# First layer's expert products: whole forms in place of half forms, and one nested branch in place of two

## The chip, the cores and the metric

One core of a Trainium2 chip runs the whole program in one launch. The metric is the device time of the launch in microseconds (us); the times shown are medians of repeated executions, and the profile is that of one further execution.

## The reference, cut to what matters

A backbone of two layers over 512 rows of width 1024 (256 context rows and 256 rows of the stream). Each layer is a mixer followed by a mixture of 16 experts, of which each token takes two:

```python
def moe(t, w_router, b_router, w1, w3, w2):          # t: (N, 1024); N = 512 in the first layer, 256 in the second
    ...                                               # gates: (N, 16), two of them not zero in a row
    y = jnp.zeros(t.shape, jnp.float32)
    for e in range(N_EXPERTS):
        h = jax.nn.silu(t @ w1[e]) * (t @ w3[e])      # w1, w3: 1024 x 512
        y = y + gates[:, e:e + 1] * (h @ w2[e])       # w2: 512 x 1024
    return y.astype(t.dtype)
```

All in float32. Only the experts of the first layer (l = 0) are changed.

## The kernel before

**Stages.** The program runs the first mixer, the first layer's experts, the second mixer and the second layer's experts, one after the other. In the trace the first layer's experts run from 538 to 893 us.

**An expert's tokens.** A router counts the tokens of each expert on the chip and writes into `cni` how many groups of 32 each expert has (`nu`). The tokens of an expert are gathered 64 to a unit: the first unit always, the second if `nu > 2` (more than 64 tokens), the third if `nu > 4` (more than 128). GpSimd (POOL) gathers the rows into `xg` (units one and two) and `xo` (unit three) and scatters the results `ys` and `yo` to `y_d`.

**Products.** `up` multiplies a unit's transposed rows by the gate and up matrices into one PSUM bank `hp`: 16 matmuls of 64 columns by 512. `down` multiplies the hidden rows by the down matrix into `yp`: 8 matmuls. `up32` and `down32` are the half forms for a unit that holds 32 tokens or fewer: 32 and 16 matmuls of 32 by 256, which fill the four column groups of the array. `zeros` clears a bank with one bf16 matmul, so that the later code may read a bank whose unit is empty. `unit_up` and `unit_down` do the third unit: transposes of `xo`, the product, the hidden rows in `yo`, then transposes, the product and the copy to `yo`.

**Branches.** `nu` is read into a register of TensorE (PE), ScalarE (ACT) and VectorE (DVE), and `tc.If` makes each of these engines branch by itself. Both sides of every branch stand in each engine's code, whether they run or not; an engine that skips a side jumps over it. One expert of the first layer has these branches in the PE code: L1733 and L1734 (third unit's up), L1724 and L1725 (second unit's up), L1749 and L1750 (second unit's down), L1756 and L1757 (copies, empty on PE), L1767 and L1768 (third unit's down).

**The loop.** For each expert `n`, in the order `SEQ`, `first_up(n)` and then `then_down(n - 1)` are written; in the first layer the order of an engine's instructions is left to a scheduler, which mixes them. PE, ACT, DVE and POOL each run their own list in order.

**Weights.** Each expert has six tiles of 1 MB. SyncE (SP) issues the loads (L1410) into a ring of 14 tiles (`wx`, `wm`, `w`): a load waits until PE has used up the tile that lay in its place, and for the load issued three before it. The ring thus holds two experts and a third of the next.

The lines of the loop that the change does not touch, but that the argument uses:

```python
                    nus[n] = count(SEQ[n], PE, ACT, DVE)
                    hs = first_up(n, xTs.pop(0), nus[n])
...
                    hT = hpose(bank(), before, "hT")
...
                    xTs.append(xpose(xg[(n + 1) % 3]))
...
                    then_down(n - 1, hT, nus[n - 1])
```

## Time and profile before

| | |
|---|---|
| median of 3 runs | 1534.67 us (1533.02 to 1538.39) |
| the profiled execution's own time | 1538.6 us |
| its span, first to last instruction | 1536.8 us |
| mean granted clock of TensorE | 0.909 of full speed |
| first layer's experts | 538 to 893 us of the span |

The span is cut into stages below. Busy time of PE counts matmuls, and "idle before" is the time in which an engine did nothing ahead of an instruction, with what ended it. `PEq` names PE's own sequencer, which is where a branch runs; "issue" is a wait for nothing that the profile shows. The queue `instruction` of the DMA table is what the engines' code is fetched with.

### The profile page before, as it was taken

The page shows a single profiled execution, that of the slowest core. Times are in us where ns is not written, and L with a number is a line of the kernel's source. Part 1 is how long each engine was busy: PE and PEld are TensorE (multiplying, and loading weights), DVE is VectorE, ACT ScalarE, POOL GpSimd, SP SyncE. Part 2 cuts the span into 40 slices and gives each one's busy share as a digit, 9 for nine tenths or more (in the row PEclk, how much of TensorE's full clock was granted, in tenths as well). Part 3 has the DMA queues.
Part 4 walks back from the last instruction along what each step waited for, and adds up shares of the span by engine and source line. Part 5 has one row for each costly group of instructions (what it writes and reads, how often), then busy time and mean ns, then how long its engine had stood idle before and what let it go on. Part 6 is the DMA issues. An engine that isn't in the chain of part 4 may idle for free. (4 is left out here: it accounts for less than half of the span.)

```text
span 1536.8 us, 21725 instructions
## 1 busy us (share of the span) xinstructions
PE 1242.1 (81%) x8336; PEld 779.4 (51%) x8336; DVE 641.0 (42%) x1581; ACT 408.3 (27%) x838; POOL 100.7 (7%) x135
## 2 busy tenths in 40 slices
PE   4899999999979278788798824899987588888873
PEld 2667887567669223333243303888647234443441
DVE  4333323455447711211112128835556445444445
ACT  2223223344343010111111113443122233333222
POOL 0000000100010210111110010000010000000000
PEclk9899999999679689999899965899998799999997
DMA  8565655600020897899988242321274879998831
GB/s 277 185 205 166 231 182 195 186 1 1 1 83 15 297 339 283 296 362 334 302 287 292 103 138 82 118 80 61 76 267 164 314 283 385 355 336 321 320 122 57
DMA packets 152139, 311.20 MB, mean 202 GB/s; under 512 B 7580, under 2 KB 39516, under 8 KB 151944
## 3 DMA queue, kind: packets, MB, share of 16 engines
q1 hardware_dynamic: 146176, 296.44, 55.2%
q0 software_dynamic: 4608, 8.59, 2.1%
q10 hardware_dynamic: 1160, 3.48, 0.6%
q8 instruction: 133, 2.18, 0.6%
q14 instruction: 62, 0.51, 0.1%
HBM read 303.24 MB, written 9.44 MB: 203 GB/s over the span
## 5 line engine op out<-in xcount | busy, mean ns | idle before, releaser
L364 PE MATMUL mm<-wh,uT 128*128 128x256 f32 (+2 forms) x960 | 194.7, 298 | 7.7 <-ACT uT L345 4.5
L364 PEld LDWEIGHTS mm<-wh,uT 128*128 128x128 f32 x960 | 159.9, 199 | 20.9 <-issue 9.9
L364 PE MATMUL mm<-wl,uT 128*128 128x256 f32 (+2 forms) x480 | 142.2, 297 | 3.8 <-DVE wl L347 3.7
L1554 PE MATMUL mm<-wx,xT 128*64 128x512 f32 x392 | 121.0, 632 | 20.0 <-PEq L1733 18.6
L364 PEld LDWEIGHTS mm<-wl,uT 128*128 128x128 f32 x480 | 95.5, 199 | 5.6 <-DVE wl L347 5.1
L347 DVE TENSOR_TENSOR wl<-w,wh 128x2048 fp32r<-128x2048 f32 (+3 forms) x33 | 53.8, 1646 | 71.3 <-ACT wh L345 45.8
L1554 PEld LDWEIGHTS mm<-wx,xT 128*64 128x64 f32 x392 | 37.8, 144 | 75.1 <-issue 71.6
L246 PE MATMUL mm<-w,sT 128*32 128x512 f32 x384 | 59.5, 632 | 11.8 <-DVE sT L210 10.3
L345 ACT CAST wh<-w 128x2048 fp32r<-128x2048 f32 (+3 forms) x33 | 45.8, 1388 | 67.0 <-DMA w<-in_w_in_even_dram 52.9
L364 PE MATMUL mm<-uT,wh 128*128 128x512 f32 (+1 forms) x208 | 58.9, 370 | 4.9 <-ACT wh L345 4.9
L1582 PE MATMUL mm<-wx,hT 128*64 128x512 f32 x168 | 51.8, 609 | 12.3 <-PEq L1767 7.2
L1567 ACT ACTIVATE hs<-mm 64x512 f32<-64x512 f32 x32 | 18.8, 589 | 151.2 <-PE mm L1554 115.7
L364 PE MATMUL mm<-wo,mx 128*128 128x256 f32 x384 | 51.4, 293 | 5.7 <-ACT wo L345 3.5
L364 PEld LDWEIGHTS mm<-wo,mx 128*128 128x128 f32 x384 | 48.7, 198 | 6.6 <-ACT wo L345 3.9
L1554 PE MATMUL mm<-w,xT 128*64 128x512 f32 x104 | 45.1, 650 | 1.1 <-issue 0.9
L1554 PE MATMUL mm<-wm,xT 128*64 128x512 f32 x80 | 41.3, 698 | 5.2 <-PEq L1733 5.2
L1608 DVE COPY ys<-mm 64x512 f32<-64x512 f32 x18 | 12.5, 693 | 78.9 <-ACT ys L1608 67.8
L364 PEld LDWEIGHTS mm<-uT,wh 128*128 128x128 f32 (+1 forms) x208 | 36.3, 184 | 14.0 <-ACT wh L345 5.2
L1568 DVE TENSOR_TENSOR hs<-hs,mm 64x512 f32<-64x512 f32 x32 | 22.1, 690 | 49.7 <-ACT hs L1567 49.3
L1494 PE MATMUL ac<-h,sel 128*64 128x512 f32 x104 | 27.3, 644 | 18.7 <-DVE sel L1485 18.7
L1117 PE MATMUL tr<-cst,yk 128*128 128x128 f32 x32 | 6.0, 350 | 44.4 <-ACT yk L1110 44.4
L1554 PE MATMUL tr<-wx,xT 128*64 128x512 f32 x152 | 39.0, 595 | 3.3 <-PE ac L1510 2.8
(472 smaller groups left out, 2341.2 us busy)
## 6 DMA issues: line engine op xcount, KB each, us to landing
w<-in_w_ada_dram SPq DMA_DIRECT2D x48, 1024.0 KB
wx<-in_w_expert_gate_dram SPq DMA_DIRECT2D x46, 1024.0 KB
wx<-in_w_expert_up_dram SPq DMA_DIRECT2D x44, 1024.0 KB
wx<-in_w_expert_down_dram SPq DMA_DIRECT2D x39, 1024.0 KB
w<-in_w_expert_down_dram SPq DMA_DIRECT2D x15, 1024.0 KB
w<-in_w_in_even_dram SPq DMA_DIRECT2D x13, 1024.0 KB
w<-in_w_expert_up_dram SPq DMA_DIRECT2D x12, 1024.0 KB
wm<-in_w_expert_down_dram SPq DMA_DIRECT2D x10, 1024.0 KB
```

What stands on the lines that cost most here:

```text
L246: nc.tensor.matmul(ps[32 * g:32 * g + 32, :], sT[:, k, :], ws[k // 4][:, k % 4, :], start=k < 4, stop=k >= 4, skip_group_check=True, tile_ ...
L345: nc.scalar.copy(hi, src)
L347: nc.vector.tensor_tensor(lo, src, hi.bitcast(FP), op=OP.subtract)
L364: nc.tensor.matmul(ps, lhs(i, k), rhs(j, k), start=(k == 0 and n == 0), stop=(k == nk - 1 and n == 2))
L1117: nc.tensor.transpose(ps[:, k * 128:(k + 1) * 128], y[:, kk_ * 128:(kk_ + 1) * 128], ident)
L1494: nc.tensor.matmul(xp[i * 64:i * 64 + 64, :], sel[:, b, :], u[:, i * 512:(i + 1) * 512], start=b == 0, stop=b == len(us) - 1, skip_group_c ...
L1554: nc.tensor.matmul(hp[i * 64:i * 64 + 64, :], xT[:, k, :], ws[2 * i + k // 4][:, k % 4, :], start=k == 0, stop=k == 7, skip_group_check=Tr ...
L1567: nc.scalar.activation(hs, hp[0:64, :], AF.Silu)
L1568: nc.vector.tensor_tensor(hs, hs, hp[64:128, :], op=OP.mult)
L1582: nc.tensor.matmul(yp[n * 64:n * 64 + 64, :], hT[:, k, :], ws[4 + k // 2][:, k % 2, n * 512:(n + 1) * 512], start=k == 0, stop=k == 3, ski ...
L1608: (nc.vector.tensor_copy if n else nc.scalar.copy)(ys[:, ns], yp[rs_, :])
```

## The change

In the first layer, `up32` and `down32` are no longer used: a unit is either left out or multiplied in whole. `zeros(hp[1])` is now done for every expert ahead of the branch. One branch `nu > 2` holds the second unit's product and, inside it, a branch `nu > 4` with the third unit; the down side has the same shape, with the copies in the same branch. The second layer's branches are the same as before, written inside its own `else`. `unit_up` and `unit_down` keep their half form as an option that the first layer no longer uses.

```diff
@@ first_up
                 hp = [(bank if l else mmt)() for _ in range(2)]
+                hs = e2p.tile([128, 512], FP, name="hs", tag="hs", bufs=2)
                 if l == 0:
+
+                    zeros(hp[1])
                     up(hp[0], xT[0], ws)
+                    with tc.If(nu > 2):
+                        up(hp[1], xT[1], ws)
+                        with tc.If(nu > 4):
+                            unit_up(n % 2, e, 2, ws)
                 else:
...
-                with tc.If(nu > 2) as c1:
-                    with tc.If(nu > 3) as c2:
-                        up(hp[1], xT[1], ws)
-                    with c2.Else():
-                        up32(hp[1], xT[1], ws)
-                with c1.Else():
-                    zeros(hp[1])
-                hs = e2p.tile([128, 512], FP, name="hs", tag="hs", bufs=2)
-                if l == 0:
-                    with tc.If(nu > 4) as c1:
-                        with tc.If(nu > 5) as c2:
-                            unit_up(n % 2, e, 2, ws)
...
-                            unit_up(n % 2, e, 2, ws, True)
...
@@ then_down
                     down(yp[0], hT[0], ws)
                     rows_out(ys[0:64, :], yp[0])
-                    downs()
-                    outs(nu)
-                    with tc.If(nu > 4) as c1:
-                        with tc.If(nu > 5) as c2:
+                    with tc.If(nu > 2):
+                        down(yp[1], hT[1], ws)
+                        rows_out(ys[64:128, :], yp[1])
+                        with tc.If(nu > 4):
                             unit_down(n % 2, e, 2, ws)
-                        with c2.Else():
-                            unit_down(n % 2, e, 2, ws, True)
```

How this moves PE's list is seen at the second expert (`n = 1`). Before, its second product stands in these rows (`mm` is a PSUM bank, `wx` a weight tile, `zb` the tile of zeros, x16 the number of equal instructions in a row):

```order
L1724 COMPARE_AND_BRANCH
L1725 COMPARE_AND_BRANCH
L1554 MATMUL mm<-wx,xT 64x512 x16
L1725 UNCONDITIONAL_BRANCH
L1458 LDWEIGHTS zb
L1458 MATMUL mm<-zb 128x256
L1562 MATMUL mm<-wx,xT 32x256 x32
L1725 UNCONDITIONAL_BRANCH
L1458 LDWEIGHTS zb
L1458 MATMUL mm<-zb 128x512
L1724 UNCONDITIONAL_BRANCH
```

The third unit's up stands a few rows ahead of that, in a branch of its own (`xo` is the third unit's gathered rows, `xT_4827` and `xT_4857` its transposes):

```order
L1733 COMPARE_AND_BRANCH
L1734 COMPARE_AND_BRANCH
L1651 MATMUL ac<-cst,xo 128x64 x8
L1554 MATMUL tr<-wx,xT_4827 64x512 x16
L1734 UNCONDITIONAL_BRANCH
L1651 MATMUL ac<-cst,xo 128x64 x8
L1458 LDWEIGHTS zb
L1458 MATMUL ac<-zb 128x256
L1562 MATMUL ac<-wx,xT_4857 32x256 x32
L1734 UNCONDITIONAL_BRANCH
L1733 UNCONDITIONAL_BRANCH
```

In the changed kernel the same expert's rows, the clearing matmul first, are these (L1722 is now `nu > 2`, L1724 `nu > 4`):

```order
L1458 LDWEIGHTS zb
L1458 MATMUL mm<-zb 128x512
L1554 MATMUL mm<-wx,xT 64x512
L1626 UNCONDITIONAL_BRANCH
L1554 MATMUL mm<-wx,xT 64x512 x2
L1710 TENSOR_LOAD cni_3546
L1722 COMPARE_AND_BRANCH
L1724 COMPARE_AND_BRANCH
L1651 MATMUL ac<-cst,xo 128x64 x8
L1554 MATMUL ac<-wx,xT_4710 64x512 x16
L1724 UNCONDITIONAL_BRANCH x2
L1554 MATMUL mm<-wx,xT 64x512 x16
```

An expert of 64 tokens or fewer jumped twice on the up side, over 8 + 16 + 8 + 32 product matmuls and then over 16 + 32; it now jumps once, over 8 + 16 + 16. On the down side of the first expert, the changed kernel has these rows of PE (L1765 is `nu > 2`, L1768 `nu > 4`, `hT` the transposed hidden rows):

```order
L1582 MATMUL mm<-wx,hT 64x512
L1765 COMPARE_AND_BRANCH
L1768 COMPARE_AND_BRANCH
L1574 MATMUL ac<-cst,yo 128x64 x4
L1582 MATMUL tr<-wx,hT 64x512 x4
L1582 MATMUL tr<-wm,hT 64x512 x4
L1768 UNCONDITIONAL_BRANCH x2
L1582 MATMUL mm<-wx,hT 64x512 x4
L1582 MATMUL mm<-wm,hT 64x512 x4
L1765 UNCONDITIONAL_BRANCH x2
```

There was a jump over 8 + 16 matmuls (L1749), an empty branch (L1756) and a jump over 4 + 8 + 4 + 16 (L1767); there is now one jump over 4 + 8 + 8.

## Rows read from the trace of the kernel before

**Rows 1.** The experts' stage: busy us (count) of PE, PEld, DVE, ACT, POOL; clock, DMA, GB/s.
```profile
538.00:893.00 355.00, 294.68 (x1672) 115.66 (x1672) 64.35 (x99) 44.74 (x81) 39.84 (x43) 0.94 0.81 281
```

**Rows 2.** Waits of PE, 538 to 893 us: total, times, longest.
```profile
PE mm L1554 <- PEq L1733: 23.8, 9, 5.5
...
PE mm L1582 <- PEq L1767: 8.5, 12, 2.4
PE mm L1458 <- issue: 4.8, 2, 3.2
PE mm L1582 <- PEq L1733: 4.4, 1, 4.4
...
PE mm L1582 <- PEq L1749: 2.5, 5, 0.6
...
PE mm L1458 <- DVE ys L1608: 2.1, 1, 2.1
...
PE mm L1554 <- DMA wx<-in_w_expert_down_dram: 0.7, 1, 0.7
```

**Rows 3.** Branches on PE's sequencer: shortest/median/longest ns, first and last start.
```profile
L1733 PEldq COMPARE_BRANCH  x16: 65/2106/6497, 539.2 to 871.5; - x16
...
L1724 PEldq COMPARE_BRANCH  x16: 70/1418/5247, 540.8 to 865.0; - x16
...
L1767 PEldq COMPARE_BRANCH  x16: 65/219/3797, 570.1 to 889.6; - x16
```

**Rows 4.** PE in order of time: start, us, what, count, [idle before].
```profile
577.00 2.64 PE L1582 MATMUL mm<-wm,hT 128*64 128x512 f32 x5 [4.42 <-PEq L1733]
...
585.47 1.06 PE L1554 MATMUL mm<-w,xT 128*64 128x512 f32 x1
...
610.44 3.66 PE L1562 MATMUL ac<-wx,xT 128*32 128x256 f32 x64 [0.57 <-DVE xT L1653]
...
625.13 0.59 PE L1554 MATMUL mm<-wm,xT 128*64 128x512 f32 x1
...
625.56 0.59 PE L1554 MATMUL mm<-wm,xT 128*64 128x512 f32 x1
...
649.44 1.93 PE L1590 MATMUL ac<-w,hT 128*32 128x256 f32 x32 [1.41 <-DVE hT L1576]
```

**Rows 5.** PE matmuls by shape, 538 to 893 us: count, busy, mean ns.
```profile
L1554 PE MATMUL mm<-wx,xT 128*64 128x512 f32 x392 | 121.0, 632 | 20.0 <-PEq L1733 18.6 <-DMA wx<-in_w_expert_down_dram 0.7 <-ACTq L1733 0.3
...
L1554 PE MATMUL mm<-w,xT 128*64 128x512 f32 x104 | 45.1, 650 | 1.1 <-issue 0.9
L1554 PE MATMUL mm<-wm,xT 128*64 128x512 f32 x80 | 41.3, 698 | 5.2 <-PEq L1733 5.2
...
L1458 PE MATMUL mm<-zb 128*128 128x512 bf16 x10 | 4.1, 409 | 7.5 <-issue 4.8 <-DVE ys L1608 2.1 <-PE mm L1554 0.7
...
L1458 PE MATMUL mm<-zb 128*128 128x256 bf16 x4 | 1.1, 283 | 0.0
...
L1458 PE MATMUL ac<-zb 128*128 128x256 bf16 x2 | 0.6, 283 | 0.0
```

**Rows 6.** DMA queues, 538 to 893 us: packets, MB, share of 16 engines.
```profile
q1 hardware_dynamic: 38010, 91.26, 72.4%
...
q8 instruction: 49, 0.80, 0.9%
```

**Rows 7.** The longest of the waits of SP's loads, 538 to 893 us.
```profile
SPq L1410 <- PE mm L1554: 83.9, 39, 10.6
```

**Rows 8.** Two stretches in which loads follow each other closely; columns as in rows 1.
```profile
660.00:680.00 20.00, 14.99 (x61) 5.74 (x59) 3.46 (x5) 2.34 (x4) 3.66 (x4) 0.91 1.04 382
...
700.00:720.00 20.00, 16.29 (x121) 6.57 (x120) 3.46 (x5) 2.34 (x4) 2.84 (x3) 1.00 0.97 324
```

**Rows 9.** The last load of the stage, from SP's list in order of time.
```profile
847.09 0.37 SPq L1410 DMA_DIRECT2D w<-in_w_expert_down_dram  x1
```

**Rows 10.** The same kind of wait in the second layer's experts, 1205 to 1500 us.
```profile
PE ac L1458 <- issue: 12.8, 5, 4.0
```

## Prediction

> **What bounds the kernel now.** I first cut the span into stages. The change touches one of them, the first layer's experts, 355 us long: PE is busy 295 us there, DVE 64, ACT 45, and the DMA engines 81% of the time at 281 GB/s [rows 1]. So it is PE or the weights, and the reader is to see which of them waits for the other. The list of PE's waits answers: for weights PE waited once, 0.7 us [rows 2]. The loads wait the other way round, 83.9 us in 39 waits for PE to finish the up products that read the tile in their place [rows 7]. PE sets the pace, the DMA engines have some room.

> PE is not busy all that time, and its waits have one author. 23.8 and 4.4 us end at branch L1733, 8.5 at L1767, 2.5 at L1749 [rows 2]. Two further entries are the same thing under another name: the clearing matmul L1458 stands right behind branch L1724, and its 4.8 us "issue" and the 2.1 us put down to a DVE copy are times in which L1724 was still being taken. Together 46.1 us. The branch view shows what a branch costs on PE's sequencer: 0.2 us in the median at L1767, but 2.1 us in the median and 6.5 at worst for L1733, 5.2 at worst for L1724 [rows 3]. These are the jumps over the longest pieces of code.

> What a long jump waits for is seen in the DMA view. In the trace a float32 product matmul is two matmul and two weight-load records, a transpose one of each. An expert's up side lays down 16 + 64 + 16 + 2 + 128 = 226 such instructions in the third unit's branch and 64 + 2 + 128 + 2 = 196 in the second's; the down side 32 + 64 = 96 and 8 + 32 + 8 + 64 = 112; what always runs is 16 + 64 + 8 + 32 = 120. That is 750 an expert, 12000 in the stage, against 49 packets of 0.80/49 MB = 16 KB on the queue that fetches code [rows 6]: one fetch for each 245 instructions, so the whole code is fetched in its order, run or not. 49 fetches in 355 us are one in 7.2 us, and a jump pair L1733, L1724 moves 400 instructions on, more than a whole fetch, in a few microseconds. PE then stands until the next piece is there.

> [...]

> **Part one: the products grow.** Half forms ran six times: four second units and two third units, seen in the six half clears of a bank [rows 5], one in each of six experts. A half up takes 3.66 us by the timeline for its 64 records, say 3.6, and 0.28 for its clear [rows 4, 5]. In a whole one, two records run side by side and pairs start 0.43 us apart (625.13 and 625.56) [rows 4], so 16 pairs take 6.9 us. A half down took 1.93 us [rows 4], a whole one is 8 pairs, 3.4 us. So each of the six costs 6.9 - 3.9 + 3.4 - 1.9 = 4.5 us more, 27 us in all. `zeros` now also runs in the six experts that did without a whole clear: 6 x 0.41 = 2.5 us [rows 5]. Sum +29.5 us of PE at full clock, all on the path, since PE sets the pace. The copies of the whole forms (two in place of four) are ACT's and DVE's, which are busy 45 and 64 us of 355 [rows 1]; I price them at nothing, and at one 0.7 us copy at the very end of the stage if that cover is gone.

> **Part two: the jumps shrink.** In the changed list an expert lays down 16 + 64 + 64 = 144 instructions in the up branch, 8 + 32 + 32 = 72 in the down branch and 122 that always run, 338 in all, 5400 in the stage: by 245 a fetch some 22 fetches, one in 15 us, against a worst wait of 6.5. An up-side jump moves 144 on, a down-side jump 72, and with the always-run instructions between them a pair stays below one fetch. So a jump finds its target there, nearly always. What stays is the price of a near jump: some 0.2 us for each of 16 at L1722 (the median of L1767 is 0.22 [rows 3]) and 0.5 us at L1765 for the ten experts that skip it (L1749's 2.5 us in 5 [rows 2]), 8 us together. Gain: 46 - 8 = 38 us. Bounds: 46 if even these vanish, and 0 if the jumps go on waiting as before.

> **Part three: the clock.** [...] The means of the three up groups, 632, 650 and 698 ns [rows 5] against 590 undisturbed (0.59 in the timeline), give (392 x 42 + 104 x 60 + 80 x 108)/470 = 67 records at half clock, each holding its slot 0.215 us longer: 14 us. The granted clock of 0.94 [rows 1] bounds it above: 12% of 355 us at half clock, 43 us, costs at most 21. The few records at the stage's start stay slow; the down products, which I leave out, have some too. Value taken: 14, of 0 to 21.

> **Sum.** 29.5 - 38 - 14 = -22.5 us. The profiled execution took 1538.6 us, its span 1536.8; it would be 1516. The median of the runs shown is 1534.7, 0.25% lower, and I make the forecast on that: 1512. Ahead of the stage only the first clearing matmul moves, into a time in which PE waits for the router; behind it nothing changes its order and all starts earlier by as much. But the second layer's code lies at other addresses, and its five waits of this kind, 12.8 us [rows 10], may as well be 7 or 19.

> **Rivals.**
> - *More than the sum.* All 46 us of waits and all 21 of the half clock go: 29.5 - 46 - 21 = -37.5, 1497 us. For it speaks that every long idle of PE is of this kind; against it, that a branch always costs something.
> - *The weights become the pace.* The stage moves 281 x 355 = 99.8 MB; the last load is issued at 847 us [rows 9], lands near 852, and 41 us of work follow. At 382 GB/s [rows 8] the traffic would fit into 261 us and would end at 799, far ahead of need; at 324 GB/s, the slacker stretch, into 308 us, to 846: a gain of 6 us, 1529. That stretch, too, has loads waiting for PE, so it is a low reading.
> - *Half of the waits stay*, because single jumps still fall on the edge of a fetched piece soon after another one: 23 of 46 and 7 of 14 go, 29.5 - 23 - 7 = 0, 1534 us.
> - *Distance is not the cause* (the other side). If the branch at the head of the up side waits for being taken at that place, whatever it jumps over, L1722 inherits L1733's 28.2 us; only L1724's 6.9, 5 of the down side's 11 and 3 of the half clock go: 29.5 - 14.9 = +14.6, 1549 us. It decides as soon as L1722's median stays near 2 us. The pattern of code fetches speaks against it. [...]

> **How the numbers follow.** The sum as it stands 0.52 (own range 1503 to 1521), more than the sum 0.15, weights 0.12, half the waits 0.12, distance not the cause 0.09. A measurement of this kernel can tell about 0.3%, 4.6 us, from no change. Faster than 1530: 0.52, 0.15, 0.09 of the weights and 0.02 of the halves, 0.78. Within 0.3%: 0.11. Slower: 0.11. The range runs from below the second case to near the half-waits case, 1494 to 1531; it leaves out the last case and the outer parts of its neighbours, some 0.2.

> **What the changed profile would show.** Packets on the code queue in the stage fall from 49 to about 22. L1722 and L1765 stand in PE's branch view with medians of a few tenths; PE's waits put down to branches fall from 46 to about 8 us. No L1562 or L1590 is left in the stage, and there are six more whole products of each kind and 16 clears. The stage's granted clock rises above 0.97. Its length falls from 355 to about 332 us, SP's waits for PE shrink, and PE still waits for weights only some microseconds. The prediction is wrong if L1722 keeps waits of 3 to 6 us (then 1534 or 1549), if PE's waits for DMA grow beyond 15 us (then 1529), or if the stage shrinks as said and the second layer's experts give it back at their own branches.

## The result, and the profile after

The changed kernel takes 1498.84 us in the median (1497.33 to 1500.31), beside 1536.53 us (1533.02 to 1539.77) for the kernel before: a ratio of 0.9755, 95% interval 0.9727 to 0.9783, or 37.7 us less. A second, later comparison gave 0.9778 (0.974 to 0.9816). The forecast was 1512, 22.5 us less. The profiled execution took 1497.3 us, with a span of 1495.5.

The stage of the first layer's experts, from the start of its first transpose to the end of its last product (busy us and count of PE, PEld, DVE, ACT, POOL; then clock, DMA share, GB/s):

```profile
534.20:857.20 323.00, 308.73 (x1383) 116.13 (x1383) 63.10 (x92) 43.34 (x73) 39.90 (x43) 0.99 0.87 308
```

The window of [rows 1] is 0.7 us wider than the stage; cut in the same way, 538.5 to 892.8 us, the stage before is 354.3 us long with PE busy for 294.7. So it is 31.3 us shorter now. PE's idle time, length minus busy, goes from 59.6 to 14.3 us (-45.3), while its busy time grows from 294.7 to 308.7 (+14.0). The granted clock rises from 0.94 to 0.99. PE's waits in the stage (total, times, longest):

```profile
PE tr L1545 <- DMA xg<-u_d,io: 9.3, 1, 9.3
PE tr L1545 <- DVE hT L1576: 3.5, 10, 0.3
...
PE mm L1554 <- PEq L1722: 1.3, 7, 0.3
PE mm L1582 <- PEq L1765: 1.2, 7, 0.2
PE mm L1582 <- ACTq L1768: 0.8, 1, 0.8
...
PE mm L1582 <- PEq L1768: 0.5, 3, 0.2
...
PE mm L1554 <- PEq L1724: 0.3, 2, 0.2
```

The first line is the wait for the first gathered rows, ahead of the stage's first transpose. The five entries at branches sum to 4.1 us, where [rows 2] had 46.1, and no wait for a weight tile is left. The branches themselves on PE's sequencer (shortest/median/longest ns):

```profile
L1722 PEldq COMPARE_BRANCH  x22: 70/181/417, 536.6 to 834.9; - x22
...
L1724 PEldq COMPARE_BRANCH  x8: 65/196/419, 579.2 to 828.8; - x8
...
L1765 PEldq COMPARE_BRANCH  x22: 65/180/431, 556.5 to 853.6; - x22
```

The longest is 0.43 us, where [rows 3] had 6.5. The up and down products by shape (count, busy, mean ns):

```profile
L1554 PE MATMUL mm<-wx,xT 128*64 128x512 f32 x504 | 143.3, 600 | 1.6 <-PEq L1722 0.8 <-PEq L1724 0.3 <-PE mm L1554 0.2
...
L1554 PE MATMUL mm<-w,xT 128*64 128x512 f32 x120 | 47.0, 595 | 0.3 <-PEq L1722 0.2 <-issue 0.2
L1554 PE MATMUL mm<-wm,xT 128*64 128x512 f32 x80 | 34.6, 596 | 0.5 <-PEq L1722 0.3 <-issue 0.2
```

The means of 632, 650 and 698 ns [rows 5] are now 595 to 600: almost no record runs at half clock, a granted clock of 0.50, which stands in 5 of the stage's 323 us (1.00 in the rest). The code queue in the stage, packets and MB, and SP's waits for its loads:

```profile
q8 instruction: 23, 0.38, 0.5%
```

```profile
SPq L1410 <- DMA wx<-in_w_expert_down_dram: 48.1, 16, 5.1
SPq L1410 <- DMA wx<-in_w_expert_up_dram: 42.7, 18, 3.0
SPq L1410 <- PE mm L1554: 36.6, 19, 9.5
```

23 code packets stand in place of 49 [rows 6]. The loads wait less for PE (36.6 us against 83.9 in [rows 7]) and now mostly for earlier loads, at 308 GB/s against 281. They keep up, though with less room.

**What lies outside the stage.** The profiled spans differ by 41.3 us. By the first and last PE work of each part, the experts' stage gives 31.3 of them (354.3 to 323.0 us). It starts 4.3 us earlier (538.5 to 534.2), and the stretch from its end to the second layer's experts is 6.6 us shorter (311.8 to 305.2); the second layer's experts take 310.1 us against 309.6. Neither gain stands in edited code. A second profile of the changed kernel has its stage start at 529.5 and that stretch at 308.2, so both move by 3 to 5 us between executions of one kernel.

### The profile page after: what moved, and what is told of

Same layout as the page of the kernel before. It is cut to its first block, busy times and chain, and to the rows that moved or that the text cites. A ratio compares the mean times of both kernels' runs of the same rounds, so it can differ in the third digit from the quotient of the medians.

```text
span 1495.5 us, 20846 instructions
## 1 busy us (share of the span) xinstructions
PE 1240.5 (83%) x8048; PEld 766.7 (51%) x8048; DVE 639.0 (43%) x1575; ACT 408.7 (27%) x832; POOL 101.2 (7%) x135
## 5 line engine op out<-in xcount | busy, mean ns | idle before, releaser
L364 PE MATMUL mm<-wh,uT 128*128 128x256 f32 (+2 forms) x960 | 189.7, 293 | 7.9 <-ACT uT L345 4.8
L364 PEld LDWEIGHTS mm<-wh,uT 128*128 128x128 f32 x960 | 155.6, 194 | 21.0 <-issue 9.9
L1554 PE MATMUL mm<-wx,xT 128*64 128x512 f32 x504 | 143.3, 600 | 1.6 <-PEq L1722 0.8
L1554 PEld LDWEIGHTS mm<-wx,xT 128*64 128x64 f32 x504 | 44.4, 137 | 66.7 <-issue 65.9
L1582 PE MATMUL mm<-wx,hT 128*64 128x512 f32 x192 | 54.1, 597 | 1.7 <-PEq L1765 0.9
L1554 PE MATMUL mm<-w,xT 128*64 128x512 f32 x120 | 47.0, 595 | 0.3 <-PEq L1722 0.2
L1554 PE MATMUL tr<-wx,xT 128*64 128x512 f32 x152 | 39.0, 595 | 3.2 <-PE ac L1510 2.8
L364 PE MATMUL mm<-uT,wl 128*128 128x512 f32 (+1 forms) x104 | 37.8, 367 | 2.3 <-DVE wl L347 2.3
```

Of the source, the lines that this page charges most:

```text
L364: nc.tensor.matmul(ps, lhs(i, k), rhs(j, k), start=(k == 0 and n == 0), stop=(k == nk - 1 and n == 2))
L1554: nc.tensor.matmul(hp[i * 64:i * 64 + 64, :], xT[:, k, :], ws[2 * i + k // 4][:, k % 4, :], start=k == 0, stop=k == 7, skip_group_check=Tr ...
L1582: nc.tensor.matmul(yp[n * 64:n * 64 + 64, :], hT[:, k, :], ws[4 + k // 2][:, k % 2, n * 512:(n + 1) * 512], start=k == 0, stop=k == 3, ski ...
```

## Experiments

The theory: a branch costs what PE waits for code, and that grows with the code that an expert lays down, run or not. A first rival says that the merged, nested branch is what helps; a second that it is the number of branches. The table gathers PE's side of the stage, each from one windows row between the start of the stage's first transpose and the end of its last product. The code length is the count of PE's instructions in the kernel's list, both sides of every branch included.

| kernel | PE instructions in the stage's code | code packets | stage, us | PE busy | PE idle |
|---|---|---|---|---|---|
| before | 12,766 | 49 [rows 6] | 354.3 | 294.7 | 59.6 |
| changed | 5,788 | 23 | 323.0 | 308.7 | 14.3 |
| e1, whole forms, old branches | 5,871 | 22 | 324.1 | 306.4 | 17.7 |
| e2, half forms, nested branch | 12,640 | 49 | 349.1 | 302.2 | 46.9 |
| e3, changed + dead code | 12,638 | 49 | 403.0 | 341.2 | 61.8 |
| e5, changed + less dead code | 7,935 | 31 | 351.4 | 317.4 | 34.0 |

**Whole forms under the old branches (e1).** Against the kernel before, the first layer's half forms are taken out, and the separate branches and the `Else` with the clear stay:

```diff
+                if l == 0:
+                    with tc.If(nu > 2) as c1:
+                        up(hp[1], xT[1], ws)
+                    with c1.Else():
+                        zeros(hp[1])
+                else:
...
-                    with tc.If(nu > 4) as c1:
-                        with tc.If(nu > 5) as c2:
-                            unit_up(n % 2, e, 2, ws)
-                        with c2.Else():
-                            unit_up(n % 2, e, 2, ws, True)
+                    with tc.If(nu > 4):
+                        unit_up(n % 2, e, 2, ws)
```

> Whole products as in the change, but the two separate branches of the kernel before (second unit with its clear in an else, third unit in a branch of its own, copies in a branch of their own). Theory 'length of code jumped over': the stage's code is as short as in the change (about 5900 instructions), so the long waits are gone here too; 1497 to 1504 us, PE's branch waits under 12 us. Rival 'the one nested branch does it': most of the gain is missing, 1515 to 1535 us, with waits of some microseconds at the branches.

Measured: 1499.26 us (1491.53 to 1504.73) beside 1531.21, ratio 0.9804 (0.9751 to 0.9858), which overlaps the changed kernel's. The up side's branches:

```profile
L1739 PEldq COMPARE_BRANCH  x18: 70/208/413, 533.0 to 833.4; - x18
...
L1725 PEldq COMPARE_BRANCH  x22: 70/178/342, 534.7 to 833.2; - x22
```

Two separate branches an expert on the up side, and none takes longer than 0.42 us. Over the whole stage PE's waits at branches sum to 11.0 us, 8.0 of them in ten waits of at most 1.0 us at the third unit's branch on the down side (L1772), where the changed kernel has 4.1 in all. The nesting may save some of that, but the time is the same without it: it is not what the change lives on.

**The nested branch with the half forms kept (e2).** The other half of the change alone, shown against the changed kernel:

```diff
                     with tc.If(nu > 2):
-                        up(hp[1], xT[1], ws)
+                        with tc.If(nu > 3) as c2:
+                            up(hp[1], xT[1], ws)
+                        with c2.Else():
+                            up32(hp[1], xT[1], ws)
                         with tc.If(nu > 4):
-                            unit_up(n % 2, e, 2, ws)
+                            with tc.If(nu > 5) as c3:
+                                unit_up(n % 2, e, 2, ws)
+                            with c3.Else():
+                                unit_up(n % 2, e, 2, ws, True)
```

> The one nested branch of the change, but with the half forms of the kernel before inside it. Theory 'length of code jumped over': 12600 instructions of code as before, one jump of 434 for an expert of 64 tokens or fewer; the waits stay (35 to 60 us of PE idle at branches, 45 or more fetches of code), and the cheaper products come back: 1525 to 1545 us. Rival 'nested branch': fewer branches and cheaper products, 1470 to 1505 us.

Measured: 1536.9 us (1529.1 to 1545.8) beside 1531.21, ratio 1.0042 (1.0012 to 1.0071): no gain. Branches on PE's sequencer, then PE's waits:

```profile
L1722 PEldq COMPARE_BRANCH  x16: 70/4661/7196, 535.3 to 853.0; - x16
...
L1771 PEldq COMPARE_BRANCH  x16: 70/420/6638, 569.0 to 876.4; - x16
```

```profile
PE mm L1554 <- PEq L1722: 22.7, 8, 5.0
...
PE mm L1582 <- PEq L1771: 4.9, 1, 4.9
PE mm L1554 <- PEq L1727: 4.9, 4, 2.0
```

The same branch L1722 that takes 0.18 us in the changed kernel takes 4.7 us in the median here, where it jumps over 434 instructions in place of some 152. (In the one profile the stage is 5.2 us shorter than before, while the median is 0.4% longer. In that profile the second layer's experts, whose source is the same, take 317.4 us in place of 309.5.)

**Dead code in the changed kernel (e3).** A half up and half down product of the second and third unit stand behind a branch that is never taken. Every product and clear that runs is the changed kernel's:

```diff
                     with tc.If(nu > 2):
                         up(hp[1], xT[1], ws)
                         with tc.If(nu > 4):
                             unit_up(n % 2, e, 2, ws)
+                    with tc.If(nu > 15):
+                        up32(hp[1], xT[1], ws)
+                        unit_up(n % 2, e, 2, ws, True)
```

(and the same with `down32` and `unit_down` on the down side)

> The change with the half forms put back as code that never runs (a branch nu > 15 behind each side, which no expert of these inputs takes), so that products and order are those of the change and the code is as long as before (12600 instructions). Theory 'length of code jumped over': 40 to 60 us of waits at the new branch come back, and the half clock behind them; 1540 to 1570 us, slower than the kernel before. Rival 'running the half forms is what cost' (their four column groups, their copies): 1499 to 1504 us.

Measured: 1578.04 us (1570.23 to 1590.68) beside 1531.21, ratio 1.029 (1.0227 to 1.0353): some 80 us more than the changed kernel took, for code that never runs, and above the 1540 to 1570 us expected. The profiled execution was the slowest of the four (1590.68 us). The stage, PE's waits in it, and its code packets:

```profile
535.20:938.20 403.00, 341.16 (x1383) 123.00 (x1383) 63.11 (x92) 44.17 (x75) 40.04 (x43) 0.93 0.72 248
```

```profile
PE mm L1554 <- PEq L1726: 32.8, 12, 8.1
PE mm L1582 <- PEq L1773: 9.7, 13, 2.5
...
PE mm L1554 <- issue: 7.8, 2, 4.1
PE mm L1582 <- issue: 2.4, 1, 2.4
```

```profile
q8 instruction: 49, 0.80, 0.8%
```

Idle time is back at 61.8 us, near the 59.6 of before, with the same 49 code packets. The busy time also grows, by 32.4 us against the changed kernel, for the same 1383 matmul records. This growth is what the expectation had too small. PE in order of time behind one such wait (start, us, what, count, [idle before]) shows why:

```profile
643.35 1.08 PE L1554 MATMUL mm<-wm,xT 128*64 128x512 f32 x1 [6.74 <-PEq L1726]
643.36 1.12 PE L1554 MATMUL mm<-wx,xT 128*64 128x512 f32 x1
644.23 1.06 PE L1554 MATMUL mm<-wm,xT 128*64 128x512 f32 x1
...
648.50 0.74 PE L1554 MATMUL mm<-w,xT 128*64 128x512 f32 x1
...
649.07 0.59 PE L1554 MATMUL mm<-w,xT 128*64 128x512 f32 x1
```

For 5 us after the wait a record takes 1.06 us in place of 0.59. In the trace of the kernel before, records of 1.06 us stand where the granted clock is 0.50 (578.00 to 579.50 us) and records of 0.59 us where it is 1.00 (624 to 627 us). So this wait of 6.7 us costs about 2.5 us more behind it (an estimate: half of those 5 us). It is the part that a count of the waits alone leaves out.

**Less dead code (e5).** Only the half up product of the second unit stands behind the never-taken branch:

```diff
+                    with tc.If(nu > 15):
+                        up32(hp[1], xT[1], ws)
```

> The changed kernel with a shorter piece of code that never runs: in each of the first layer's 16 experts a half up product of the second unit behind a branch that is never taken (132 instructions of PE by my count, jumped over 16 times, beside the 151 of the changed kernel's own up-side jump); the stage's code grows from some 5800 to some 7900 instructions, about 32 fetches in place of 23. What is computed is that of the changed kernel. Code-length theory: the two jumps of an expert together pass more than one fetched piece (284 against 245), so part of the waits comes back, but each jump is short of one piece: PE's waits at branches in the stage 10 to 30 us against the changed kernel's 3, the time 1510 to 1540 us on a chip where the kernel before takes 1531 to 1537. Rival one, that only a jump of more than a whole piece costs (as 280 did in the earlier run with dead code): within 5 us of the changed kernel, 1494 to 1504. Rival two, that one more branch an expert is what costs, whatever its length: the same as the earlier run with dead code, 1570 to 1590.

Measured: 1526.13 us (1518.73 to 1529.41) beside 1533.79, ratio 0.9945 (0.9919 to 0.9971), 27 us more than the changed kernel on the same chip. Both rivals fall. The stage, the two jumps of the up side, their waits, and the code packets:

```profile
532.40:883.80 351.40, 317.40 (x1383) 116.99 (x1383) 63.10 (x92) 43.37 (x74) 39.83 (x43) 0.97 0.81 283
```

```profile
L1722 PEldq COMPARE_BRANCH  x22: 70/182/367, 534.8 to 861.1; - x22
...
L1726 PEldq COMPARE_BRANCH  x16: 208/270/4632, 536.5 to 861.3; - x16
```

```profile
PE mm L1554 <- PEq L1726: 18.2, 12, 5.0
...
PE mm L1554 <- issue: 2.7, 2, 1.7
```

```profile
q8 instruction: 31, 0.51, 0.6%
```

L1722 jumps over the same 151 to 154 instructions as in the changed kernel and is as quick. L1726 jumps over only 132 to 134, fewer than L1722, and yet holds the waits: it comes right behind, and the two together move 284 instructions on, more than one packet (256 instructions here, 7,935 in 31). In e3 a branch at the same place jumps over 280 instructions in place of 132, and its waits are 32.8 us in place of 18.2. In e1, too, two up-side jumps follow each other, over 83 and 66 instructions, and PE's waits at them stay at 0.3 us or less. What counts in these runs is the code passed in a short time, not one branch's distance and not the number of branches.

**The second layer's second unit whole (e4).** The same recipe on the other layer, on top of the change:

```diff
-                    with tc.If(nu > 2) as c1:
-                        with tc.If(nu > 3) as c2:
-                            up(hp[1], xT[1], ws)
-                        with c2.Else():
-                            up32(hp[1], xT[1], ws)
-                    with c1.Else():
-                        zeros(hp[1])
+                    zeros(hp[1])
+                    with tc.If(nu > 2):
+                        up(hp[1], xT[1], ws)
```

(and `down` and `rows_out` alone under `nu > 2` in `downs` and `outs`)

> The change, and in the second layer the second unit without half form too, its bank cleared ahead of the branch; the jump over it falls from 198 instructions to 66. Theory 'length of code jumped over': the waits behind that branch (12.8 us in the kernel before) and their half clock go, one product of a half form grows by 4.5 us: 1483 to 1494 us. Rival: those waits are another cost of a branch there, or are hidden by the loads: 1499 to 1504 us.

Measured: 1490.32 us (1485.8 to 1491.62) beside 1531.21, ratio 0.9725 (0.9673 to 0.9778), against the change's 0.9755 in another comparison: the intervals overlap. So both ran again, side by side on one chip:

> The changed kernel itself, for a comparison with the next on one chip. Expected 1497 to 1501 us where the kernel before takes 1531 to 1537.

> The kernel with the second layer's second unit made whole, beside the changed kernel on one chip. If its gain is real (its waits of 8.2 us behind that branch are gone): 7 to 10 us below the changed kernel. If the earlier 8.5 us came from the chips and the executions: within 3 us of it.

Measured: the changed kernel 1499.44 us (1494.16 to 1506.6), this one 1484.71 us (1479.64 to 1488.29), with ratios of 0.9778 (0.974 to 0.9816) and 0.967 (0.9637 to 0.9703). The gain is real: 14.7 us, more than the 7 to 10 expected. The second layer's experts in the two profiles, the changed kernel first:

```profile
1160.40:1473.60 313.20, 257.93 (x1927) 126.78 (x1927) 136.39 (x330) 94.80 (x210) 0.00 (x0) 0.95 0.77 283
```

```profile
1163.50:1463.40 299.90, 256.90 (x1880) 123.23 (x1880) 136.09 (x328) 94.68 (x210) 0.00 (x0) 0.98 0.80 295
```

The stage is 13.3 us shorter, nearly all of it idle time (55.3 to 43.0), in a stage where the code falls from 11,071 to 7,900 instructions. The second unit's branch, L1731 in the first profile of the changed kernel and L1732 in the first of this one:

```profile
L1731 PEldq COMPARE_BRANCH  x16: 70/1324/5880, 1173.2 to 1452.6; - x16
```

```profile
L1732 PEldq COMPARE_BRANCH  x18: 70/210/3442, 1176.5 to 1445.9; - x18
```

How much of this gain comes from the shorter jumps alone is not separated from where the code happens to lie. The seven profiles that hold the second layer's code unchanged have that stage at 305.6 to 318.3 us (310.1 and 313.2 in the two of the changed kernel), the two profiles of this version at 299.9 and 300.7.

**No half form anywhere (e6).** On top of e4, the second layer's first unit is whole too:

```diff
-                    with tc.If(nu > 1) as c0:
-                        up(hp[0], xT[0], ws)
-                    with c0.Else():
-                        up32(hp[0], xT[0], ws)
+                    up(hp[0], xT[0], ws)
```

(and the same on the down side)

> The kernel with the second layer's second unit made whole, with the first unit of the second layer made whole too: no half form is left in the kernel. Eleven half up and eleven half down products that ran there become whole ones. By the price of the prediction, 4.5 us each, PE gets 49 us of product work more in a stage where it waits for no weights, and the branches that were left there cost next to nothing now: 1490 + 49 = about 1539 us, 1525 to 1545. Rival, that the half forms cost more in code and branches than they save in the second layer as well: 1490 or less.

Measured: 1529.09 us (1522.8 to 1538.83), 44 us more than the version with the halves on the same chip. The second layer's experts:

```profile
1168.20:1506.00 337.80, 304.29 (x1390) 121.42 (x1390) 133.07 (x308) 95.90 (x210) 0.00 (x0) 0.98 0.71 260
```

PE's busy time grows by 304.3 - 256.9 = 47.4 us, or 4.3 for each of the eleven pairs of half products made whole, and 9.5 us of idle time go. Where half forms run in eleven of sixteen experts they earn far more than their code costs.

## Why the prediction was right, and where its sum was short

The mechanism was right, and the time lies in the range. The sum for the stage was -22.5 us and the stage gave -31.3. Its terms, with what they measured:

| term | predicted, us | measured, us | from |
|---|---|---|---|
| six half products whole, six more clears | +29.5 | about +28.3 | 6 x 4.3 (e6) and 6 x 0.41 [rows 5] |
| waits for code | -38 | -42.0 at branches, -45.3 of idle time in all | 46.1 to 4.1; 59.6 to 14.3 |
| records at half clock | -14 | about -14 | busy +14.0, less the 28.3 above |

**Products.** 4.5 us a pair was the price; 4.3 came out, in a stage that e6 makes longer. They were on the path, as PE set the pace.

**Waits.** This is the mis-sized term: "What stays is the price of a near jump ... 8 us together". Some 4 us of it stayed (the five entries above). About 3 more went that had not been put down to code at all: waits of 2.3 and 0.9 us marked "issue" in the straight-line products at L1582 and L1554 of the kernel before. In the changed kernel's list the first is gone and 0.3 us of the second is left. That they were waits for code is inferred, not shown: e3 and e5, where nothing but dead code was added, bring "issue" entries back (7.8, 2.4 and 2.7 us).

**Half clock.** The size was right, and the worked means of [rows 5] were a fair guide. The 470 ns that they were divided by are 1.06 less 0.59 us, the slow record at 585.47 us and the quick one at 625.13 [rows 4]; slow pairs there start 0.85 us apart (584.62, 585.47, 586.33), quick ones 0.43. The granted clock of the kernel before is 0.50 from 585.00 to 586.50 us and 1.00 from 624 to 627 us; from 500 to 900 us it is one or the other in all but 17 of 1600 quarters of a microsecond. Slow records followed the 4.42 us wait at 577 us [rows 4] (1.06 us at 578.65), by 583.45 a record took 0.59 again, and the one at 585.47 came after a second wait, of 2.1 us:

```profile
578.65 1.06 PE L1554 MATMUL mm<-wm,xT 128*64 128x512 f32 x1
...
582.67 0.38 PE L1458 MATMUL mm<-zb 128*128 128x512 bf16 x1 [2.10 <-DVE ys L1608]
...
583.45 0.59 PE L1554 MATMUL mm<-w,xT 128*64 128x512 f32 x1
```

What the prediction did not see is how strong this term becomes with more waits: PE's busy time grows by 32.4 us in e3. The half clock's own share of that is about 25 us, an estimate from the granted clock (0.93 over 403.0 us against 0.99 over 323.0).

**The rivals.** *More than the sum* gave the time that came (1497 forecast, 1499 measured), though partly for another reason: idle -45 is its -46, but the half clock gave back 14 rather than its 21, and the stage explains 31.3 of the 37.7 us. The last 6 or so lie outside it, where the same kernel differs by as much from one execution to the next; whether the moved code has a share in the stretch behind the stage (310.1 to 312.7 us in the three kernels with 49 packets, 304.3 to 309.2 in the seven profiles with fewer) is open. *Weights become the pace* did not happen: no wait for a tile, though the loads' rate rose to 308 GB/s. *Half of the waits stay* is what e5 looks like. *Distance is not the cause* is refuted twice: L1722 stands where L1733 stood and takes 0.18 us, and in e2, with the half code under it, 4.7. The change's own second layer neither gave nor took anything (310.1 us against 309.6), its five waits being 8.2 us in place of 12.8 [rows 10].

**What fetches the code.** The instruction list lets the fetch count be checked more closely than the 245 of the prediction: 5,788, 7,935 and 12,638 instructions came in 23, 31 and 49 packets (the changed kernel, e5, e3), which is 252, 256 and 258 to a packet, and 252 to 267 over the six kernels of the table. How much code lies ready for PE was not shown. In e5 passing 284 instructions, 1.1 packets, already waits for up to 5.0 us, where the jump over 151 to 154 takes 0.18 us in the median; whether it matters where in its packet the branch stands was not followed up. The jumps over 200 to 434 instructions in the kernel before and in e2 wait for up to 7.2 us.

What limits the fetches was not tried. Whether they would come sooner with fewer weight loads in flight is open.

## What to carry to other kernels

In this kernel a specialised form behind a branch cost every iteration its code, also where it never ran (some 80 us in e3), so set the time that it saves where it runs (4.3 us a pair, as measured in the second layer; six experts of the first layer and eleven of the second have one) against what its code makes all iterations wait. Add up the instructions that an engine can jump over in a short stretch, two branches in a row included, and compare them with one code packet (252 to 267 instructions here): below it the branches here took 0.2 us in the median, above it waits of up to 5.0 us (e5) and 8.1 us (e3) came. The version that dropped the rarely used half forms in both layers and kept the often used ones was the fastest of those run, at 1484.7 us.

## What the hardware showed that was not expected

```profile
L1798 PEldq COMPARE_BRANCH  x2: 3291/3550/3810, 854.2 to 1472.1; - x2
```

Over the whole span the queue of the code packets above moved 106. PE's list of 34,026 instructions would be 133, at the 256 to a packet of e5, and without what these two jumps pass 103. So, by this count, they alone save fetches, and cost less than the 7.2 us that a jump over 434 instructions took at worst in e2.

A wait's price does not end with it: in e3 47.5 us more of idle time than in the changed kernel came with 32.4 us more of busy time for the same matmuls, most of it at half clock by the estimate above (25 us), and in e5 19.7 us came with 8.7.
